# Output layers whose accumulators are added straight into the residual, and low parts made by ScalarE and an accumulating DMA

## The chip, the core and the metric

One NeuronCore of a Trainium2 chip runs one launch of the kernel. Its engines each run their own instruction stream in order: TensorE (PE; its weight loads are PEld), VectorE (DVE), ScalarE (ACT), GpSimd (POOL) and SyncE (SP, which here only issues DMAs). SBUF is the on-chip memory, PSUM holds matmul results, DRAM tensors hold inputs and spilled data. The metric is the device time of one launch in microseconds.

## The reference

One inference layer, on 1024 prompt tokens and 8 sample tokens together (1032 columns), model width 1024, in float32:

```python
x = layer_norm(ALPHA * x + 0.5 * swiglu(x, ffn1_wi, ffn1_wo), ln_g[0], ln_b[0])
...  # projections, mLSTM, short convolution, mixing: x <- LN2(...)
x = layer_norm(ALPHA * x + 0.5 * swiglu(x, ffn2_wi, ffn2_wo), ln_g[2], ln_b[2])
x = layer_norm(ALPHA * x + jax.nn.sigmoid(x @ w_pg) * (p @ w_pp), ln_g[3], ln_b[3])

def swiglu(x, wi, wo):
    g, u = jnp.split(x @ wi, 2, axis=-1)
    return (jax.nn.silu(g) * u) @ wo
```

The hidden width is 2816, that is 22 blocks of 128. The change concerns the second product of both SwiGLUs, `(...) @ wo`, called the output layer here.

## The kernel before

**Numbers in two pieces.** PE's matmuls take operands rounded to a shorter float (`fp32r`), so each operand is split: a high part, the rounded value, and a low part, value minus high part. A product is three matmuls: high times high, high times low, low times high (lines L432, L433, L434 of `product`; L172 to L174 in `unit`, the plain products). The low part of the activations is first needed by L433.

**Seven products for eight.** Most matrix products go by a Strassen-like scheme: a 256 x 256 weight block and two column halves of the data make seven products of sums instead of eight. `wcomb` forms the seven weight operands (copies of the high part on ACT, L258; low parts on DVE, L259; the sums on DVE, L267 and L270, and on POOL, L268 and L275). `pair` runs the seven products, j = 0 to 6, for each of two column strips s (256 and 260 columns), into PSUM accumulators: `mm` (four), `aux` (three), and one `pn` that `unit_ps` hands out every fifth time. Accumulator A takes products 0, 2 and 5, E takes 4 and 6; 1 and 3 go to `aux` tiles. Of A after 0, A after 2, product 3 and E after 4 a snapshot is copied to the SBUF tile `sreg` by ACT (L450, L457, L461, L465), and each of the four results per strip is a DVE sum of a snapshot and an accumulator (L454, L469, L470, L474).

**The output layer** in `ffn`. The hidden activations of eight (layer 1) or nine (layer 2) pairs of 128-blocks have been spilled as seven combined operands each, in the DRAM tensor `hsum`; a few blocks stay plain in `hscr`. Pairs are taken in groups of three (one group of two in layer 1). For a group, 7 x 3 = 21 *parts* of 128 x 516 are loaded by `split_load`: SP's DMA into the low half of a tile (L587), ACT's rounding copy to the high half (L588), DVE's subtraction (L589) in place over the low half. Then four `segment`s run, one for each 256 output rows: load `wo` (L603), `wcomb`, and `pair`. `out` has DVE write a result into a `tmp` tile and POOL add that to the residual tile `RT` (L610). Layer 1 has 8 pairs in three groups, layer 2 has 9 in three: 24 segments. The tiles of the parts are reused: product 0's parts of the next group may be loaded when PE has finished product 0 of the group's last segment, and so on, and in the next group they serve one product later. After the groups come the plain blocks (`ounit`, L632).

Every engine's order is fixed when the kernel is built: a list scheduler simulates the program and appends each instruction to its engine's stream, and an instruction waits for the semaphores of what it needs. So a late operand holds up all that stands behind it on that engine.

Of the kernel before, what the change touches and what calls it, by code (L numbers as in the profile page):

```python
# [11 lines left out]
AF = mybir.ActivationFunctionType  # L12
OP = mybir.AluOpType
# [17 lines left out]
BN = (256, 260)  # L31
BM = 260
BLK4 = [(i // 2 * HW + i % 2 * BN[0], BN[i % 2]) for i in range(4)]
# [3 lines left out]
def F_(ap):  # L37
    return ap.bitcast(F32)
# [25 lines left out]
def layer_kernel(ctx: ExitStack, tc: tile.TileContext, I, O):  # L64
    nc = tc.nc
    V, S, G, T, DQ = nc.vector, nc.scalar, nc.gpsimd, nc.tensor, nc.sync
# [28 lines left out]
    def tmp(n=BM):  # L95
        return tmpp.tile([128, BM], F32, name="tmp", tag="tmp")[:, :n]
# [6 lines left out]
    def unit_ps(n=512):  # L103

        turn["n"] += 1
        return mm(n) if turn["n"] % 5 else psp.tile([128, 512], F32, name="pn", tag="pn", bufs=1)[:, :n]
# [3 lines left out]
    def aux(n=512):  # L110
        return psp.tile([128, 512], F32, name="aux", tag="aux", bufs=7 - NMM)[:, :n]
# [71 lines left out]
    def bs(t, b, blk=BLK):  # L183
        c0, n = blk[b]
        return t[:, c0:c0 + n]
# [63 lines left out]
    def wcomb(raws):  # L249

        lo_, up = raws
        g = lo_.shape[1]
        a11, a21, a12, a22 = lo_[:, :, 0:128], lo_[:, :, 128:256], up[:, :, 0:128], up[:, :, 128:256]

        def put(src):
            s = slot()
            hi, lo = (s[:, i * 512:i * 512 + g * 128].rearrange("p (k n) -> p k n", n=128) for i in range(2))
            S.copy(hi, src)  # L258
            V.tensor_tensor(lo, src, F_(hi), op=OP.subtract)  # L259
            return hi, lo  # L260

        def fresh():
            return rawp.tile([128, 512], F32, name="raw", tag="raw")[:, :g * 128].rearrange("p (k n) -> p k n", n=128)

        s1, s2, s3 = fresh(), fresh(), fresh()
        out = [put(a11)]
        V.tensor_tensor(s1, a21, a22, op=OP.add)  # L267
        G.tensor_tensor(s3, a11, a21, op=OP.subtract)  # L268
        out.append(put(a12))
        V.tensor_tensor(s2, s1, a11, op=OP.subtract)  # L270
        out.append(put(s2))
        out.append(put(a22))
        out.append(put(s1))
        s4 = fresh()
        G.tensor_tensor(s4, a12, s2, op=OP.subtract)  # L275
        out.append(put(s3))
        out.append(put(s4))
        return out
# [150 lines left out]
    def product(ps, w, xs, start, stop):  # L429
        for kp, (xh, xl) in enumerate(xs):  # L430
            wh, wl = (t[:, kp] for t in w)
            T.matmul(ps, wh, xh, start=start and kp == 0, stop=False, skip_group_check=True)  # L432
            T.matmul(ps, wh, xl, start=False, stop=False, skip_group_check=True)  # L433
            T.matmul(ps, wl, xh, start=False, stop=stop and kp == len(xs) - 1, skip_group_check=True)  # L434
# [3 lines left out]
    def pair(ws, XS, subs, out, first=False):  # L438

        live = {}  # L440

        def step(j, s):
            w = ws[j]
            xs = XS(j, s) if callable(XS) else [xparts(XS[s], j, kp) for kp in range(4)]
            P = live.setdefault(s, {})
            snap = [SN["v"][i][s] for i in range(4)]
            if j == 0:
                P["A"] = mm(BN[s])
                product(P["A"], w, xs, True, False)
                order_["snap"] = S.copy(snap[0], P["A"]).ins  # L450
            elif j == 1:
                ps = aux(BN[s])
                product(ps, w, xs, True, True)
                out(0, s, lambda d: V.tensor_tensor(d, snap[0], ps, op=OP.add))  # L454
            elif j == 2:
                product(P["A"], w, xs, False, False)
                order_["snap"] = S.copy(snap[1], P["A"]).ins  # L457
            elif j == 3:
                ps = aux(BN[s])
                product(ps, w, xs, True, True)  # L460
                order_["snap"] = S.copy(snap[2], ps).ins  # L461
            elif j == 4:
                P["E"] = mm(BN[s])
                product(P["E"], w, xs, True, False)
                order_["snap"] = S.copy(snap[3], P["E"]).ins  # L465
            elif j == 5:
                A = P["A"]
                product(A, w, xs, False, True)
                out(1, s, lambda d: V.scalar_tensor_tensor(d, snap[2], -1.0, A, op0=OP.mult, op1=OP.add))  # L469
                out(1, s + 2, lambda d: V.tensor_tensor(d, snap[3], A, op=OP.add))  # L470
            else:
                E = P["E"]
                product(E, w, xs, False, True)
                out(0, s + 2, lambda d: V.tensor_tensor(d, snap[1], E, op=OP.add))  # L474


        for j, s in [(j, s) for js in ((0, 1), (2, 3, 4, 5, 6)) for s in subs for j in js] if first else \
                [(j, s) for j in range(7) for s in subs]:
            step(j, s)
            with tc.issue_after(order_["snap"]):  # L480
                for f in beside.pop(0) if beside else ():
                    f()

    def ffn(wi, wo, l, XS, enter, xlate, raws, sgs, RTs, res, groups, plains, tail, extra=None):
# [91 lines left out]
        for p in range(1, NHID // 2):  # L576
            for k in range(2):
                w = w0 if p == 1 and k == 0 else wcomb(wi_raw(p, k))
# [5 lines left out]
        def split_load(t, src):  # L584

            hi, lo = t
            DQ.dma_start(F_(lo), src)  # L587
            S.copy(hi, F_(lo))  # L588
            V.tensor_tensor(lo, F_(lo), F_(hi), op=OP.subtract)  # L589
            return hi, lo  # L590

        RT = []
# [5 lines left out]
        def segment(ps_, parts, n, i):  # L598
            g = len(ps_)
            rw = []  # L600
            for q in range(2):
                t = gen(raws[2 * (i % 2) + q])[:, :g * 256].rearrange("p (k n) -> p k n", n=256)
                DQ.dma_start(t, wo[ps_[0] * 256:(ps_[0] + g) * 256, n * 256:(n + 1) * 256].rearrange(  # L603
                    "(k t p) n -> t p k n", t=2, p=128)[q])
                rw.append(t)

            def out(i, c, fn):
                t, r = tmp(BN[c % 2]), bs(RT[2 * n + i], c, BLK4)
                fn(t)
                G.tensor_tensor(r, r, t, op=OP.add)  # L610

            pair(wcomb(rw), lambda j, s: [tuple(bs(u, s, BLK4) for u in parts[j, k]) for k in range(g)], (0, 1), out)

        i = 0
        for ps_, slots in groups:
            parts = {}
            for j in range(7):
                for k, p in enumerate(ps_):
                    t = gen(slots[j * len(ps_) + k], R)
# [14 lines left out]
        for gi, rows_ in enumerate(plains):  # L634
# [10 lines left out]
            else:  # L645
                if extra:
                    r = ring["slots"][ring["i"] % 9:] + ring["slots"][:ring["i"] % 9]
# [102 lines left out]
    ps = aux()  # L750
# [3 lines left out]
    ps = aux()  # L754
# [170 lines left out]
    def lin_store(dst, d, n, sm):  # L925
        for i in range(2):
# [5 lines left out]
            if sm is not None:  # L932
# [6 lines left out]
    parts = {0: [(0, 26, 27), (1, 0, 1)], 2: [(7, 31, 32), (6, 10, 11)],  # L939
             1: [(0, 2, 3), (1, 8, 9)], 3: [(7, None, None), (6, 28, 29)]}  # L940
# [13 lines left out]
    for c in (0, 2, 1, 3):  # L954
        for k in range(2):
            for i in range(2):
                if len(wp) < 4:
                    wp.append(wcol(w_in, (Q0, K0)[k] + i * 128))
                ps = unit_ps(BLK4[c][1])
# [477 lines left out]
    ps = aux()  # L1437
# [314 lines left out]
    for t, nm in ((gB, "ln_g"), (bB, "ln_b")):  # L1752
        src = I[nm][0, 3]
# [61 lines left out]
```

## Time and profile before

| | us |
|---|---|
| median of 3 runs | 2705.56 (2703.46 to 2705.6) |
| the profiled execution | 2706.57 |
| its span, first to last instruction | 2704.8 |
| PE busy | 2647.3 (98%) |
| DVE busy | 1856.5 (69%) |
| ACT busy | 1341.6 (50%) |
| POOL busy | 830.1 (31%) |

All stretches below are microseconds from the span's start. Layer 1's output layer runs from about 461 to 645, layer 2's from about 2317 to 2515. In the groups of instructions, a row has line, engine, operation, tiles (out<-in, numbers left out), shapes and count, then the busy time, the mean ns of one, and the idle time of that engine just before with what ended it. In a row of one line's instructions stand the minimum, median and maximum in ns and the first and last start. In the table by stretches each engine has its busy time and, in brackets, its number of instructions; then PE's granted clock, the share of DMA and its GB/s. A wait's row has the total, the number and the longest. Matmuls overlap in their pipeline, so their rate is read from counts, not from the duration of one.

### The profile page before, as it was taken

What the parts mean: (1) busy time and instruction counts of PE and PEld (TensorE: products, weight loads), DVE (VectorE), ACT (ScalarE), POOL (GpSimd) and SP (SyncE); (2) the same over time, 40 slices, a digit from 0 to 9 for tenths busy, and PEclk for the clock granted to TensorE, in tenths of its full rate; (3) what the DMA queues carried; (4) which work ended last, traced back from release to release, by engine and by line L of the source; (5) the groups of instructions that cost most, each with busy time, mean ns of one, the idle gap of its engine ahead of it and who ended that gap; (6) DMA issues with size and microseconds to landing.
All of it is one profiled execution on the core that took longest, in us unless ns stands there. A gap on an engine that the chain in (4) does not pass through costs nothing.

```text
span 2704.8 us, 56720 instructions
## 1 busy us (share of the span) xinstructions
PE 2647.3 (98%) x21775; PEld 2610.3 (97%) x21775; DVE 1856.5 (69%) x3932; ACT 1341.6 (50%) x3031; POOL 830.1 (31%) x840
## 2 busy tenths in 40 slices
PE   9999999999999999999999999999999999999998
PEld 9999999999999999999999999999999999999888
DVE  6755556887885756646666677758855555788887
ACT  5544446554554445446666555425544444655351
POOL 2222221565421111111111334323322222465554
PEclk9999999999999999999999999999999999999999
DMA  6333236432332434236657776731433323643211
GB/s 206 103 108 107 89 104 209 145 120 69 102 107 88 122 98 126 79 88 181 183 176 230 244 231 220 249 100 32 161 100 106 102 90 109 214 150 119 81 46 58
DMA packets 311928, 355.18 MB, mean 131 GB/s; under 512 B 28536, under 2 KB 246344, under 8 KB 311656
## 3 DMA queue, kind: packets, MB, share of 16 engines
q1 hardware_dynamic: 289336, 330.30, 38.4%
q10 hardware_dynamic: 22320, 21.26, 2.7%
q8 instruction: 170, 2.79, 0.4%
q14 instruction: 102, 0.84, 0.1%
HBM read 246.09 MB, written 105.42 MB: 130 GB/s over the span
## 4 chain that ended last, share of the span: by engine, by line
PE 37%; DVE 6%; DMA 4%; issue 2%; ACT 2%; POOL 1%; SPq 0%; DVEq 0%; ACTq 0%; POOLq 0%
PE mm L432 5%; PE mm L433 5%; PE mm L434 5%; PE mm L172 4%; PE mm L174 4%; PE mm L173 4%; PE aux L433 2%; PE aux L434 2%; PE aux L432 2%; PE pn L174 1%; PE pn L172 1%; DMA a<-in_w_in_dram 1%; PE pn L173 1%; DVE a L212 1%; DMA a<-yscr 1%
## 5 line engine op out<-in xcount | busy, mean ns | idle before, releaser
L432 PE MATMUL mm<-a,w 128*128 128x256 f32 (+1 forms) x2402 | 680.5, 284 | 9.4 <-DVE tmp L470 5.9
L433 PE MATMUL mm<-a,w 128*128 128x256 f32 (+1 forms) x2402 | 676.8, 282 | 1.2 <-DVE a L212 1.2
L434 PE MATMUL mm<-a,w 128*128 128x256 f32 (+1 forms) x2402 | 675.2, 281 | 0.0
L432 PEld LDWEIGHTS mm<-a,w 128*128 128x128 f32 x2402 | 452.6, 188 | 15.9 <-DVE tmp L470 7.6
L433 PEld LDWEIGHTS mm<-a,w 128*128 128x128 f32 x2402 | 453.0, 189 | 2.1 <-DVE a L212 1.6
L434 PEld LDWEIGHTS mm<-a,w 128*128 128x128 f32 x2402 | 452.6, 188 | 0.1
L275 POOL TENSOR_TENSOR raw<-a,raw 128x512 f32<-128x512 f32 (+2 forms) x98 | 125.4, 1279 | 949.5 <-issue 443.9
L259 DVE TENSOR_TENSOR w<-raw,w 128x512 fp32r<-128x512 f32 (+2 forms) x258 | 185.6, 721 | 203.5 <-ACT w L258 201.1
L432 PE MATMUL aux<-a,w 128*128 128x260 f32 (+1 forms) x1000 | 283.1, 283 | 3.9 <-DVE a L454 3.0
L433 PE MATMUL aux<-a,w 128*128 128x260 f32 (+1 forms) x1000 | 282.1, 282 | 0.0
L434 PE MATMUL aux<-a,w 128*128 128x260 f32 (+1 forms) x1000 | 282.1, 282 | 0.0
L432 PE MATMUL mm<-a,e 128*128 128x256 f32 (+1 forms) x812 | 230.1, 283 | 1.6 <-DVE tmp L474 1.1
L433 PE MATMUL mm<-a,e 128*128 128x256 f32 (+1 forms) x812 | 229.0, 282 | 0.8 <-DVE a L212 0.8
L434 PE MATMUL mm<-a,e 128*128 128x256 f32 (+1 forms) x812 | 228.6, 281 | 0.0
L610 POOL TENSOR_TENSOR a<-a,tmp 128x256 f32<-128x256 f32 (+1 forms) x192 | 178.9, 959 | 86.8 <-DVE tmp L454 37.8
L174 PE MATMUL mm<-a,w 128*128 128x256 f32 (+4 forms) x715 | 201.5, 285 | 0.0
L172 PE MATMUL mm<-a,w 128*128 128x256 f32 (+3 forms) x671 | 191.7, 287 | 4.0 <-ACT w L148 1.7
L432 PEld LDWEIGHTS aux<-a,w 128*128 128x128 f32 x1000 | 188.9, 189 | 5.4 <-DVE a L454 4.0
L258 ACT CAST w<-a 128x512 fp32r<-128x512 f32 (+2 forms) x200 | 117.5, 587 | 149.7 <-PE mm L434 93.6
L173 PE MATMUL mm<-a,w 128*128 128x256 f32 (+3 forms) x671 | 190.6, 285 | 0.0
L434 PEld LDWEIGHTS aux<-a,w 128*128 128x128 f32 x1000 | 189.1, 189 | 0.0
L433 PEld LDWEIGHTS aux<-a,w 128*128 128x128 f32 x1000 | 189.1, 189 | 0.0
(508 smaller groups left out, 7790.9 us busy)
## 6 DMA issues: line engine op xcount, KB each, us to landing
a<-in_ffn_wi_dram SPq DMA_DIRECT2D x80, 512.0 KB
a<-in_w_in_dram SPq DMA_DIRECT2D x68, 512.0 KB
a<-hsum SPq DMA_DIRECT2D x119, 258.0 KB
hsum<-a SPq DMA_DIRECT2D x68, 258.0 KB
a<-in_ffn_wo_dram SPq DMA_DIRECT2D x40, 384.0 KB
a<-in_state_C_dram ACTq DMA_DIRECT2D x32, 256.0 KB
out_dram<-a ACTq DMA_DIRECT2D x32, 256.0 KB
raw<-in_w_b_dram SPq DMA_DIRECT2D x32, 256.0 KB
```

The lines of the kernel that those rows point to most:

```text
L172: T.matmul(ps, wh, xh, start=(i == 0), stop=False)
L173: T.matmul(ps, wh, xl, start=False, stop=False)
L174: last = T.matmul(ps, wl, xh, start=False, stop=(i == n - 1))
L212: order_["lo"] = V.tensor_tensor(dst[1], src, F_(dst[0]), op=OP.subtract).ins
L258: S.copy(hi, src)
L259: V.tensor_tensor(lo, src, F_(hi), op=OP.subtract)
L275: G.tensor_tensor(s4, a12, s2, op=OP.subtract)
L432: T.matmul(ps, wh, xh, start=start and kp == 0, stop=False, skip_group_check=True)
L433: T.matmul(ps, wh, xl, start=False, stop=False, skip_group_check=True)
L434: T.matmul(ps, wl, xh, start=False, stop=stop and kp == len(xs) - 1, skip_group_check=True)
L610: G.tensor_tensor(r, r, t, op=OP.add)
```

## The change

Two edits, both in `ffn`.

1. In a segment, `pair`, `out`, `tmp`, the snapshots and POOL's adds go. Each accumulator is added straight from PSUM into the residual by DVE as it stands after each product: 8 adds for each strip, 16 for each segment (product 5's twice), with high priority. A and E come from `unit_ps`, products 1 and 3 from `aux`.
2. In `split_load` the subtraction on DVE goes. ACT writes minus the high part over the low half, and a DMA that POOL issues adds the same DRAM source to it.

```diff
             hi, lo = t
             DQ.dma_start(F_(lo), src)
             S.copy(hi, F_(lo))
-            V.tensor_tensor(lo, F_(lo), F_(hi), op=OP.subtract)
+            S.activation(lo, F_(hi), AF.Copy, scale=-1.0)
+            G.dma_start(F_(lo), src, accum_op=OP.add)
             return hi, lo
...
-            def out(i, c, fn):
-                t, r = tmp(BN[c % 2]), bs(RT[2 * n + i], c, BLK4)
-                fn(t)
-                G.tensor_tensor(r, r, t, op=OP.add)
-
-            pair(wcomb(rw), lambda j, s: [tuple(bs(u, s, BLK4) for u in parts[j, k]) for k in range(g)], (0, 1), out)
+            w = wcomb(rw)
+
+            def add(i, c, ps, op=OP.add):
+                r = bs(RT[2 * n + i], c, BLK4)
+                with tc.high_priority():
+                    V.tensor_tensor(r, r, ps, op=op)
+
+            A, E = {}, {}
+            for j, s in [(j, s) for j in range(7) for s in range(2)]:
+                if j in (0, 4):
+                    (E if j else A)[s] = unit_ps(BN[s])
+                ps = (aux(BN[s]) if j % 2 and j < 5 else E[s] if j in (4, 6) else A[s])
+                product(ps, w[j], [tuple(bs(u, s, BLK4) for u in parts[j, k]) for k in range(g)],
+                        j not in (2, 5, 6), j not in (0, 2, 4))
+                if j == 3:
+                    add(1, s, ps, OP.subtract)
+                elif j == 5:
+                    add(1, s, ps)
+                    add(1, s + 2, ps)
+                else:
+                    add(int(j == 4), s + 2 if j in (2, 4, 6) else s, ps)
```

Lines of the new kernel: L588 is still the copy of the high part, L589 is now ACT's negation, L590 POOL's DMA.

The scheduler makes another order of this. The places shown are at layer 1's first change of group (about 509 us in the profile before); `a_` numbers are tile instances, and differ between the two kernels for the same part. ACT before, from the first reused part (a_6845) on; e and w are weight operands:

```order
L588 CAST a_6845<-a_6845 128x516
L258 CAST e_6936<-a_6919 128x384
L588 CAST a_6849<-a_6849 128x516
L457 COPY sreg<-mm 128x256
L588 CAST a_6853<-a_6853 128x516
L588 CAST a_6857<-a_6857 128x516
L457 COPY sreg<-mm 128x260
L258 CAST w_6939<-raw 128x384
```

ACT now, from the same part (a_6805) on:

```order
L588 CAST a_6805<-a_6805 128x516
L589 ACTIVATE a_6805<-a_6805 128x516
L588 CAST a_6810<-a_6810 128x516
L258 CAST e_6914<-a_6897 128x384
L588 CAST a_6815<-a_6815 128x516
L589 ACTIVATE a_6810<-a_6810 128x516
L588 CAST a_6820<-a_6820 128x516
L258 CAST w_6917<-raw 128x384
L589 ACTIVATE a_6815<-a_6815 128x516
```

The snapshots (L457) are gone and the negations stand among the copies. POOL before, in the same place, has weight sums and residual adds:

```order
L275 TENSOR_TENSOR raw<-a_6919,raw 128x384
L268 TENSOR_TENSOR raw<-a_7116 128x384
L610 TENSOR_TENSOR a_5950<-a_5950,tmp 128x256 x2
L610 TENSOR_TENSOR a_5950<-a_5950,tmp 128x260 x2
L610 TENSOR_TENSOR a_5947<-a_5947,tmp 128x256
```

and now:

```order
L590 DMA a_6815<-hsum_91 128x516
L275 TENSOR_TENSOR raw<-a_6897,raw 128x384
L590 DMA a_6820<-hsum_91 128x516
L268 TENSOR_TENSOR raw<-a_7078 128x384
L590 DMA a_6825<-hsum_91 128x516
L590 DMA a_6830<-hsum_91 128x516
```

Fifteen accumulating DMAs in a row, the last two rows the first of them, stand here before POOL's next sum. PE before, at the last three reused parts (a_6905 to a_6913), product 6 of the next group's first segment:

```order
L434 MATMUL mm<-a_6901,w_6944 128x260
L432 MATMUL mm<-a_6905,w_6947 128x256
L433 MATMUL mm<-a_6905,w_6947 128x256
L434 MATMUL mm<-a_6905,w_6947 128x256
L432 MATMUL mm<-a_6909,w_6947 128x256
L433 MATMUL mm<-a_6909,w_6947 128x256
```

and now (a_6880 is the part a_6905 was; e_7105 is a weight of the second segment):

```order
L433 MATMUL mm<-a_6870,e_7105 128x256
L433 MATMUL mm<-a_6875,w_6922 128x256
L434 MATMUL mm<-a_6875,w_6922 128x256
L433 MATMUL mm<-a_6875,w_6922 128x260
L434 MATMUL mm<-a_6875,w_6922 128x260
L434 MATMUL mm<-a_6870,e_7105 128x256
L432 MATMUL mm<-a_6875,e_7105 128x256
L433 MATMUL mm<-a_6875,e_7105 128x256
L432 MATMUL pn<-a_6880,w_6925 128x256
```

PE goes through the parts one at a time, with both strips and products of the second segment in between, where it took a whole product of nine matmuls before the next.

## The prediction

> **What bounds the kernel now.** First the page: totals of each engine and the 40 slices (each 67.6 us).
>
> ```profile
> span 2704.8 us, 56720 instructions
> PE 2647.3 (98%) x21775; PEld 2610.3 (97%) x21775; DVE 1856.5 (69%) x3932; ACT 1341.6 (50%) x3031; POOL 830.1 (31%) x840
> ...
> DVE  6755556887885756646666677758855555788887
> ACT  5544446554554445446666555425544444655351
> ```
>
> TensorE (PE) is busy 98%, so the change, which leaves its matmuls as they are, can gain only idle time of PE. The output layers lie in slices 7 to 10 and 35 to 38, where VectorE (DVE) mostly reads 7 and 8. Second, the table by stretches: for each, PE's busy time and matmuls.
>
> ```profile
> core 0: us, PE busy (x) PEld busy (x) DVE busy (x) ACT busy (x) POOL busy (x), PEclk, DMA share, GB/s
> 2100.00:2150.00 50.00, 50.00 (x423) 50.00 (x422) 26.47 (x54) 20.75 (x47) 10.58 (x9) 1.00 0.27 85
> 461.00:482.00 21.00, 20.78 (x173) 20.36 (x172) 20.70 (x36) 16.42 (x35) 8.36 (x8) 1.00 0.83 297
> 505.00:545.00 40.00, 37.73 (x315) 37.31 (x314) 36.93 (x61) 24.10 (x55) 23.06 (x23) 1.00 0.55 179
> 575.00:605.00 30.00, 26.64 (x213) 25.46 (x212) 29.37 (x45) 21.11 (x49) 16.24 (x17) 1.00 0.56 194
> 605.00:645.00 40.00, 38.92 (x312) 37.35 (x313) 32.53 (x61) 18.17 (x43) 27.88 (x33) 1.00 0.34 107
> 2365.00:2396.00 31.00, 29.43 (x241) 28.65 (x240) 26.71 (x44) 20.77 (x48) 12.87 (x14) 1.00 0.64 214
> 2428.00:2460.00 32.00, 29.76 (x247) 29.35 (x247) 29.07 (x48) 21.01 (x48) 15.72 (x15) 1.00 0.60 202
> ```
>
> The first row is PE undisturbed: 50/423 = 0.1182 us per matmul. What a stretch lasts beyond its count times 0.1182 is lost: 0.5 us at the start of layer 1's output (461), 2.8, 2.5 and 2.8 us at three changes of group (505, 2365, 2428), 4.8 us at the fourth (575) and 3.1 us in layer 1's tail (605). At the changes DVE is busy 86 to 98% and DMA works hardest: the next group's parts are loaded there. The waits of PE in 500 to 645 name DVE, not DMA:
>
> ```profile
> PE mm L432 <- DVE tmp L470: 3.5, 5, 1.2
> PE mm L432 <- DVE tmp L474: 1.8, 2, 1.1
> PE aux L432 <- DVE tmp L454: 0.9, 1, 0.9
> ```
>
> So at stake is 0.5 + 8.1 + 4.8 = 13.4 us, and little of the tail's 3.1.
>
> **The evacuation.** Groups of instructions by line and shape:
>
> ```profile
> L610 POOL TENSOR_TENSOR a<-a,tmp 128x260 f32<-128x260 f32 x96 | 95.2, 1002 | 7.2 <-DVE tmp L469 4.0 <-DVE tmp L454 3.0
> L589 DVE TENSOR_TENSOR a<-a 128x516 fp32r<-128x516 f32 x119 | 95.2, 818 | 18.6 <-ACT a L588 17.8
> L461 ACT COPY sreg<-aux 128x260 f32<-128x260 f32 x98 | 37.0, 377 | 64.9 <-PE aux L434 64.1 <-issue 0.7
> L259 DVE TENSOR_TENSOR w<-raw,w 128x384 fp32r<-128x384 f32 x52 | 36.8, 711 | 18.0 <-ACT w L258 18.0
> L454 DVE TENSOR_TENSOR tmp<-sreg,aux 128x260 f32<-128x260 f32 x52 | 21.8, 419 | 9.4 <-PE aux L434 9.2
> L258 ACT CAST w<-raw 128x384 fp32r<-128x384 f32 x52 | 27.0, 520 | 19.9 <-POOL raw L275 12.8 <-DVE raw L270 7.1
> ...
> L211 ACT CAST a<-a 128x256 fp32r<-128x256 f32 x112 | 43.4, 406 | 24.6 <-DVE a L1174 22.9 <-DVE st L1093 0.6 <-PE pn L1188 0.6
> ```
>
> There are 24 segments. Each loses 8 snapshots on ScalarE (ACT), 8 DVE sums into tmp and 8 POOL adds, and gains 16 DVE adds from PSUM into the residual, priced like L454 (a PSUM and an SBUF operand, same width). ACT: 192 x 0.377 = -72 us. POOL: 192 adds at 1.0 us, -190 us. DVE: +192 x 0.419 = +80 us, and -119 x 0.818 = -97 us for the low parts that leave it. None of it lies on PE's path except where PE waited for DVE above. The new read before PE accumulates on (product 0's add before product 2) has three products between, 27 matmuls or 3.2 us for groups of three, against an add of 0.42 us; I cost it at nothing. If DVE's queue runs more than 2.8 us late that cover is gone, and DVE's load falls.
>
> **The low parts.** Per part, DVE's subtraction (0.69 us at best) becomes an ACT negation, a wait of POOL for it, and an accumulating DMA that fetches the part from DRAM a second time; SP's plain load stays. What PE now waits for is a DMA behind ACT. The rows at the first change of group, 509 to 540:
>
> ```profile
> L587 SPq DMA_DIRECT2D a<-hsum x21: 319/382/1358, 509.4 to 524.4; - x21
> ...
> L588 ACT CAST a<-a x21: 619/627/652, 513.2 to 531.1; 128x516 fp32r<-128x516 f32 x21
> ...
> L589 DVE TENSOR_TENSOR a<-a x21: 680/689/1506, 513.8 to 538.6; 128x516 fp32r<-128x516 f32 x21
> ...
> GB/s 169 307 101 296 397 312 314 360 362 322 365 373 405 386 230 233 323 260 381 341 314 280 392 392 389 187 3 11 164 301 42 0 21 0 0 0 0 0 0 0
> DMA packets 4223, 6.77 MB, mean 218 GB/s; under 512 B 384, under 2 KB 1532, under 8 KB 4220
> ```
>
> (the last two rows are DMA's rate in 40 slices of 0.775 us and its total in that stretch.)
>
> A load takes 3.8 us from issue (509.4) to ACT's copy (513.2), and DMA runs at 300 to 400 GB/s for 20 us: already full. The order of ACT after the change (shown under the change) holds two passes per part where it held one: from the first reused part's copy to the last of 18 negations it has 21 copies, 18 negations and 10 casts: 39 x 0.627 + 10 x 0.52 = 29.7 us. Begun at 513.2, that ends at 542.9; an accumulate as quick as a load (3.8 us) lands at 546.7.
>
> The scheduler has moved PE's need back too (the rows of PE under the change). PE now takes parts one at a time with the next segment's products between. From PE's release of the last reused part's slot to its first need of the low part the order had 134 matmuls and has 202. Counted from the first release (509.4) the last need is 298 matmuls on: 509.4 + 298 x 0.1182 = 544.6. So even with cheap accumulates the last part is 546.7 - 544.6 = 2.1 us late.
>
> The accumulate's price no row shows. At least it moves what a load moves, 128 x 516 x 4 bytes = 0.264 MB; at most it reads both operands one after the other and costs two loads, 0.528 MB. With two, DMA moves 6.77 + 18 x 0.528 = 16.3 MB; at 400 GB/s (the better slices) 40.7 us from 509, and 1 us to land (an estimate): 550.7, 6.1 us late. I take two: the destination must be fetched too, and DMA is full here. The Trainium skill, "Collectives: The Full Stack", section "The bandwidth ceiling: the fold count and why AG ≠ RS ≠ AR", says an adding transfer pushes two reads through the same ring and measured half the rate; no run here shows that, and it would give the same 6.1 us.
>
> Three changes of group follow this pattern: 3 x 6.1 = 18.3 us late in place of the 8.1 us lost now, **+10.2**. Start of layer 1's output, where ACT and DMA are fuller still (ACT's residual scaling, and 442 to 472):
>
> ```profile
> 442.00:472.00 30.00, 30.00 (x255) 30.00 (x254) 23.44 (x48) 25.73 (x51) 4.32 (x4) 1.00 1.00 355
> ...
> DMA packets 5109, 10.66 MB, mean 355 GB/s; under 512 B 488, under 2 KB 1514, under 8 KB 5107
> ...
> L588 ACT CAST a<-a x20: 608/627/662, 445.1 to 475.3; 128x516 fp32r<-128x516 f32 x20
> ...
> L587 SPq DMA_DIRECT2D a<-hsum x21: 319/320/339, 442.5 to 475.6; - x21
> ...
> L596 ACT ACTIVATE a<-a x16: 1067/1076/1098, 453.6 to 2337.6; 128x1032 f32<-128x1032 f32 x16
> ```
>
> PE needs the last part 351 matmuls after the first release, 442.5 + 41.5 = 484.0. DMA: 10.66 MB less 1.2 MB that is for later, plus 19 x 0.528: 19.5 MB, 48.8 us, 492.3 with landing: 8.3 us late, less 0.5, **+7.8**. ACT alone: 38 x 0.627 + 8 x 1.076 + 9 x 0.377 + 10 x 0.52 = 41.0 us from 445.1, plus 3.8: 489.9, 5.9 us late. Layer 1's second change of group (573 to 605) has 11 short and 4 double-length accumulates ahead of its need:
>
> ```profile
> DMA packets 3124, 6.39 MB, mean 200 GB/s; under 512 B 304, under 2 KB 1072, under 8 KB 3119
> ...
> L587 SPq DMA_DIRECT2D a<-hsum x11: 319/381/587, 572.0 to 584.8; - x11
> ...
> L588 ACT CAST a<-a x16: 617/633/1082, 574.7 to 592.5; 128x516 fp32r<-128x516 f32 x11, 128x1032 fp32r<-128x1032 f32 x5
> ```
>
> Without the fifth long part, which is for later, 5.9 + 11 x 0.528 + 4 x 1.057 = 15.9 MB: 39.7 us from 573, 613.7 with landing; the need is 237 matmuls after the first load's issue at 572.0, 600.0: 13.7 us late, less 4.8, **+8.9**. Layer 2's start has 366 matmuls of cover (43.3 us, 1.8 more than layer 1's) and its residual scaling (L596) runs as late as 2337.6, behind the parts: **0**. On POOL the accumulates stand in a row with the weight sums (L268, L275). The tightest is the next segment's fourth sum, behind the 19th accumulate: begun at about 543, its weight is ready by 547 (1.2 us of sum, copy and split), and PE needs it 351 matmuls after the first release, at 551: nothing. On SP, part loads stand behind weight loads that wait for these sums to free a buffer; the one among this change's loads waits only for the third accumulate: nothing. Sum: 10.2 + 7.8 + 8.9 = **+27 us**. The profiled execution took 2706.57 us, the median of the runs is 2705.56; I forecast 2706 + 27 = **2733 us**.
>
> **Rivals.** (1) No change: an accumulate costs one load. ACT alone sets lateness: 3 x 2.1 - 8.1 = -1.8; 5.9 - 0.5 = +5.4; at the second change 22 x 0.627 + 8 x 1.08 + 13 casts of 256 columns at 0.406 (L211) = 27.7 us from 574.7, plus 3.8: 606.2, 6.2 late, less 4.8 = +1.4. Sum +5, 2711; 0.2% is 5.4 us, about what a measurement here tells from nothing. The Trainium skill, "DMA: Bandwidth & Descriptors", section "Anatomy of one DMA — SWDGE (gpsimd) path", fits 2.0 us plus size over 436 GB/s for one transfer of POOL's queue: an estimate of 2.6 us where I have 3.8 from the row, by which this rival's sum would be about -1 us; no run here shows it yet.
>
> (2) Faster: the parts come in time and PE's losses go, 13.4 plus some of the tail's, -15, 2690. It decides if accumulates land within 1.7 us of their negation (544.6 - 542.9) at every change. For it: DVE's weight splits (L259) run 711 ns on average beside POOL's adds, which leave. Against it: ACT's 29.7 us at a change.
>
> (3) Much slower: POOL's issue of an accumulate is the bound. SP's issue takes 0.32 to 0.38 us, POOL's own adds 1.0; 18 issues exceed DMA's 41 us only above 1.9 us each. At 3 us: 514.4 + 54 + 3.8 = 572, 27.6 late at three changes, 25 more each, and some 20 at the other two places: +115, 2820.
>
> **How the numbers follow.** Forecast 0.42, rival 1 0.22, faster 0.15, rival 3 and accumulates of three loads (each change 18 us late instead of 6, about +80) together 0.21. The forecast's own range is 2715 to 2752. The range over the cases is 2694 to 2770: it cuts the far ends of the faster and of the much slower case. Faster by over 0.2% 0.15, within 0.2% 0.22, slower 0.63.
>
> **What would show it.** PE waits at L433 in 461 to 645 and 2317 to 2460 on a DMA into a from hsum, 5 to 14 us per change; waits on L470 gone there; ACT's L588 and L589 back to back at 513 to 543; DMA full for 40 us, not 20; bytes up by 33 to 37 MB or double that. Wrong if DMA's busy time at a change ends by 540, or if PE waits on ACT or on POOL instead.

## The result: slower, by three times the forecast

The changed kernel took 2792.06 us (median; 2788.42 to 2800.46) beside 2705.58 us for the kernel before: a ratio of 1.0325, 95% interval 1.0303 to 1.0346, 86 us slower. The forecast was 2733 us with a range to 2770. The direction was right, and so were five of the six places; the size was not, and the sixth place had been set at nothing.

The page of the new kernel (totals, PE's row of the 40 slices, and DMA's totals):

```profile
span 2791.5 us, 56628 instructions
PE 2668.3 (96%) x21775; PEld 2627.2 (94%) x21775; DVE 1795.1 (64%) x3995; ACT 1358.9 (49%) x2968; POOL 757.4 (27%) x777
...
PE   9999998888999999999999999999999999888898
...
DMA packets 330505, 391.91 MB, mean 140 GB/s; under 512 B 30601, under 2 KB 248409, under 8 KB 330233
```

PE has the same 21775 matmuls and a span 86.7 us longer; DVE has less work than before (64% where it had 69%). The six places of the prediction, by the table of stretches (the stretches are those of the new kernel's own times):

```profile
core 0: us, PE busy (x) PEld busy (x) DVE busy (x) ACT busy (x) POOL busy (x), PEclk, DMA share, GB/s
440.00:505.00 65.00, 51.06 (x382) 48.22 (x380) 24.24 (x56) 41.37 (x77) 22.43 (x25) 0.92 1.02 278
528.00:580.00 52.00, 41.37 (x302) 40.62 (x301) 23.99 (x55) 29.80 (x57) 22.44 (x25) 0.87 1.03 240
604.00:655.00 51.00, 36.81 (x275) 34.96 (x274) 24.36 (x66) 28.23 (x50) 17.79 (x21) 0.87 0.98 236
2337.00:2398.00 61.00, 46.99 (x360) 45.38 (x360) 25.18 (x58) 39.54 (x76) 24.26 (x27) 0.92 1.06 288
2423.00:2474.00 51.00, 38.91 (x296) 37.63 (x295) 22.67 (x53) 29.59 (x57) 22.40 (x25) 0.87 1.05 246
2499.00:2549.00 50.00, 40.96 (x316) 40.59 (x316) 25.74 (x59) 29.31 (x55) 21.70 (x24) 0.90 1.01 239
```

With 0.1182 us for each matmul, the rows lose 19.8, 16.3, 18.5, 18.4, 16.0 and 12.6 us: 101.6 us, where the prediction counted 13.4 before (with nothing at layer 2's start, where 515 matmuls took 61.00 us). The difference of 88 us is about the whole change of the span (86.7). The rest of the program shifts by a few us that nearly cancel: by the same matmuls, 6.8 us less are lost between the two output layers and 4.4 us more behind the second. In each row DMA's share is 0.98 to 1.06: it is full for 50 to 65 us at a time, and DVE is busy about half of that or less. The waits of PE over the whole span, longest first:

```profile
PE aux L432 <- ACT a L589: 20.2, 3, 8.1
PE mm L433 <- DMA a<-hsum: 12.3, 9, 6.2
PE mm L432 <- ACT w L258: 8.2, 3, 4.1
PE pn L432 <- DVE a L613: 7.5, 1, 7.5
PE mm L172 <- DVE a L648: 6.7, 5, 4.1
PE aux L433 <- DMA a<-hsum: 6.0, 5, 3.1
PE mm L432 <- DVE a L613: 4.8, 6, 1.7
PE aux L432 <- DVE a L613: 4.3, 5, 1.8
```

The wait that the prediction named, L433 on an accumulating transfer, is only 18 us of it. The other names are ACT and DVE: for instance a weight (L258) or a PSUM tile that DVE's add (L613) has yet to empty. A name in such a row needs care: L432 doesn't read what L589 writes. The longest wait of the table, just before 2464 us, in order of time (start and duration in us; in brackets the engine's idle time before, and what ended it):

```profile
2462.56 0.51 ACT L258 CAST cd<-a 128x384 fp32r<-128x384 f32 x1
...
2463.10 0.56 DVE L259 TENSOR_TENSOR cd<-a,cd 128x384 fp32r<-128x384 f32 x1 [13.11 <-ACT cd L258]
...
2463.58 0.75 DVE L613 TENSOR_TENSOR a<-a,aux 128x256 f32<-128x256 f32 x2
2464.14 0.55 PE L432 MATMUL aux<-a,w 128*128 128x256 f32 x1 [8.14 <-ACT a L589]
```

PE starts when DVE's add has emptied the `aux` tile. That add stood on DVE behind a weight split, the split waited 13 us for a cast on ACT, and the cast stood behind part copies (L588) that waited for their loads. The wait of 5.7 us that ended at 569.5 has the same sequence. So it looked as if standing in line on ACT made PE late; one experiment below tests it.

### The profile page after: what moved, and what is told of

It reads as the page before. It is cut to its first block, busy times and chain, and to the rows that moved or that the text cites. A ratio compares the mean times of both kernels' runs of the same rounds, so it can differ in the third digit from the quotient of the medians.

```text
span 2791.5 us, 56628 instructions
## 1 busy us (share of the span) xinstructions
PE 2668.3 (96%) x21775; PEld 2627.2 (94%) x21775; DVE 1795.1 (64%) x3995; ACT 1358.9 (49%) x2968; POOL 757.4 (27%) x777
## 2 busy tenths in 40 slices
DMA packets 330505, 391.91 MB, mean 140 GB/s; under 512 B 30601, under 2 KB 248409, under 8 KB 330233
## 3 DMA queue, kind: packets, MB, share of 16 engines
q0 software_dynamic: 18576, 36.73, 7.5%
HBM read 282.82 MB, written 105.42 MB: 139 GB/s over the span
## 4 chain that ended last, share of the span: by engine, by line
PE 71%; DMA 15%; DVE 7%; ACT 3%; issue 2%; POOL 1%; SPq 0%; ACTq 0%; DVEq 0%; POOLq 0%
PE mm L432 12%; PE mm L433 12%; PE mm L434 12%; PE aux L432 5%; PE aux L433 5%; PE aux L434 5%; PE mm L172 5%; PE mm L174 5%; PE mm L173 5%; DMA a<-hsum 3%; DMA a<-hscr 2%; DVE a L212 1%; DMA a<-in_w_in_dram 1%; PE pn L173 1%; PE pn L172 1%
## 5 line engine op out<-in xcount | busy, mean ns | idle before, releaser
L432 PE MATMUL mm<-a,w 128*128 128x256 f32 (+1 forms) x2313 | 656.3, 285 | 18.5 <-ACT w L258 8.2
L433 PE MATMUL mm<-a,w 128*128 128x256 f32 (+1 forms) x2313 | 654.3, 283 | 13.4 <-DMA a<-hsum 12.3
L434 PE MATMUL mm<-a,w 128*128 128x256 f32 (+1 forms) x2313 | 651.8, 282 | 0.0
L432 PEld LDWEIGHTS mm<-a,w 128*128 128x128 f32 x2313 | 437.2, 189 | 25.3 <-ACT w L258 8.8
L433 PEld LDWEIGHTS mm<-a,w 128*128 128x128 f32 x2313 | 438.3, 190 | 16.3 <-DMA a<-hsum 14.7
L434 PEld LDWEIGHTS mm<-a,w 128*128 128x128 f32 x2313 | 438.2, 190 | 0.1
L275 POOL TENSOR_TENSOR raw<-a,raw 128x512 f32<-128x512 f32 (+2 forms) x98 | 125.7, 1282 | 919.7 <-issue 421.5
L259 DVE TENSOR_TENSOR w<-raw,w 128x512 fp32r<-128x512 f32 (+2 forms) x258 | 177.1, 687 | 240.0 <-ACT w L258 235.5
L432 PE MATMUL aux<-a,w 128*128 128x260 f32 (+1 forms) x1000 | 284.0, 285 | 19.9 <-ACT a L589 13.9
L433 PE MATMUL aux<-a,w 128*128 128x260 f32 (+1 forms) x1000 | 283.5, 284 | 4.3 <-DMA a<-hsum 4.3
L432 PE MATMUL mm<-a,e 128*128 128x260 f32 (+1 forms) x785 | 222.6, 284 | 2.6 <-ACT a L588 2.5
L433 PE MATMUL mm<-a,e 128*128 128x260 f32 (+1 forms) x785 | 221.7, 283 | 1.0 <-DVE a L212 0.8
L434 PE MATMUL mm<-a,e 128*128 128x260 f32 (+1 forms) x785 | 221.3, 282 | 0.0
L432 PEld LDWEIGHTS aux<-a,w 128*128 128x128 f32 x1000 | 190.2, 190 | 22.1 <-ACT a L589 17.0
L174 PE MATMUL mm<-a,w 128*128 128x256 f32 (+3 forms) x739 | 208.8, 285 | 0.2 <-DVE w L149 0.2
L172 PE MATMUL mm<-a,w 128*128 128x260 f32 (+4 forms) x695 | 199.0, 287 | 6.9 <-DVE a L648 5.9
L173 PE MATMUL mm<-a,w 128*128 128x260 f32 (+4 forms) x695 | 197.8, 286 | 0.0
L433 PEld LDWEIGHTS aux<-a,w 128*128 128x128 f32 x1000 | 190.8, 191 | 5.0 <-DMA a<-hsum 5.0
L258 ACT CAST w<-a 128x512 fp32r<-128x512 f32 (+2 forms) x200 | 117.1, 586 | 157.5 <-PE mm L434 95.2
L258 ACT CAST w<-raw 128x512 fp32r<-128x512 f32 (+2 forms) x258 | 152.4, 591 | 58.6 <-PE mm L434 27.4
```

The lines of the kernel that those rows point to most:

```text
L172: T.matmul(ps, wh, xh, start=(i == 0), stop=False)
L173: T.matmul(ps, wh, xl, start=False, stop=False)
L174: last = T.matmul(ps, wl, xh, start=False, stop=(i == n - 1))
```

## The experiments

Twelve kernels, each timed beside the kernel before (medians of 2701 to 2706 us). In the comparisons of places, "lost" is worked out as above.

**Edit 1 alone.**

```diff
-            S.activation(lo, F_(hi), AF.Copy, scale=-1.0)
-            G.dma_start(F_(lo), src, accum_op=OP.add)
+            V.tensor_tensor(lo, F_(lo), F_(hi), op=OP.subtract)
```

> Edit 1 alone: accumulators are added straight into the residual, the low parts are again the subtraction on VectorE. Theory: edit 1 is harmless or a small gain, and all of the loss of 86 us sits in the low parts: at the changes of group the losses of before (2.8, 4.8, 2.5 and 2.8 us) shrink with VectorE's load, so 2690 to 2704 us. Rival: the new order of TensorE (one part at a time, two segments interleaved) is itself what makes it wait, because it needs a part's low half sooner: then 2730 us or more without any accumulating transfer.

2691.19 us, ratio 0.9953 (0.9935 to 0.9972): faster than both kernels, so the loss isn't edit 1's. The rival is not settled by this run: with the subtraction back, the scheduler doesn't make the interleaved order. By the traces, in the changed kernel 162 of the L433 matmuls don't stand right behind the L432 of their own product, here 44, in the kernel before 34. The narrow kernel below keeps that order. Two of DVE's groups (subtraction, and the 384-wide weight splits) fit the gain:

```profile
L589 DVE TENSOR_TENSOR a<-a 128x516 fp32r<-128x516 f32 x119 | 86.1, 737 | 17.0 <-ACT a L588 16.7
...
L259 DVE TENSOR_TENSOR w<-raw,w 128x384 fp32r<-128x384 f32 x52 | 28.9, 559 | 4.2 <-ACT w L258 4.2
```

737 ns for a subtraction that took 818 before, 559 for a split that took 711: without POOL's residual adds beside them, DVE's own instructions are shorter.

**Edit 2 alone.** The reverse: the kernel before, with the two lines of `split_load` from the change.

> Edit 2 alone: snapshots, tmp and GpSimd's residual adds stay, the low parts come from ScalarE's negation and the accumulating transfer. Theory: the loss of 86 us is here whole, and more, since GpSimd's adds (1.0 us each) now stand between the accumulating transfers, and ScalarE's snapshots among the passes: 2790 to 2830 us. Rival (edit 1's order of TensorE is to blame): 2750 us or less.

2804.95 us, ratio 1.0382 (1.0365 to 1.0400), 103 us over the kernel before. So the edits nearly add up: 103 - 11 is 92, and both together gave 86. The loss is edit 2's, and so is most of the new order of PE (109 L433 matmuls away from their L432).

**A plain transfer, and a narrow one.** Two kernels with everything of the change but the adding, or but the bytes:

```diff
-            G.dma_start(F_(lo), src, accum_op=OP.add)
+            G.dma_start(F_(lo), src)                                            # plain
+            G.dma_start(F_(lo)[:, 0:4], src[:, 0:4], accum_op=OP.add)           # narrow
```

> The changed kernel with GpSimd's transfer made a plain one: it overwrites the low half with the source where it added to it (the low halves are then wrong numbers). Every instruction, wait and order is the same; only the adding is gone. Theory of price: in 520 to 590 us of the changed kernel the accumulating queue held DMA for 46% of 70 us for 21 parts, 1.53 us each, against 0.66 us for a load at 400 GB/s. With a plain transfer 18 parts take 13 to 15 us less of DMA at each change, so the six places lose 50 to 60 us less in all: 2730 to 2745 us. Theory of the chain: it isn't what the transfer costs DMA, but that a second transfer stands behind copy, negation and GpSimd's issue, each part 9 us after the other: then 2775 us or more.

> The changed kernel with the accumulating transfer cut to the first 4 of 516 columns (the other columns keep minus the high part). The waits and the instructions stay, DMA's bytes for it go; the order of instructions shifts in places. Theory of price: DMA is then as free as before, ScalarE's two passes are what is left, by the working of the first rival 5 us over the kernel before or less: 2700 to 2715 us. Theory of the chain: a transfer still has to be issued by GpSimd and land after the negation, so most of the loss stays: 2750 us or more.

Plain: 2723.53 us, ratio 1.0074 (1.0059 to 1.0089). Narrow: 2681.43 us, ratio 0.9919 (0.9904 to 0.9933). The plain kernel has every instruction of the changed one in the same order, so the adding alone costs 2792 - 2724 = 68 us. The narrow one keeps all instructions and, up to shifts, the interleaved order of PE (153 L433 away from their L432); its 4 columns lie in the first strip, so only that strip's matmuls read what the transfer writes. It is the fastest kernel of the study: that order, the negation and POOL's issue cost PE next to nothing. Its row for the first change of group:

```profile
508.00:545.00 37.00, 37.00 (x314) 37.00 (x313) 25.41 (x58) 29.78 (x59) 22.40 (x25) 1.00 0.71 194
```

314 matmuls in 37.00 us are 0.1178 each: nothing lost, with ACT as busy as in the changed kernel (29.8 us) and DMA at 0.71. Apart from the second strip's wait the chain is that of the changed kernel; what differs is what DMA carries. The queue of POOL's transfers on the pages of the changed kernel and of the plain one (packets, MB, share of 16 engines):

```profile
q0 software_dynamic: 18576, 36.73, 7.5%
```

```profile
q0 software_dynamic: 10960, 36.73, 3.8%
```

The same bytes take 0.075 x 2791.5 = 209 us of all 16 engines with adding and 0.038 x 2722.6 = 103 us without: twice. With 119 single and 10 double parts that is 1.51 and 0.74 us a part. The Trainium skill, "Collectives: The Full Stack", section "The bandwidth ceiling: the fold count and why AG ≠ RS ≠ AR", says of the adding step of a reduction between cores that it reads two sources through one ring and gets half the rate; this trace agrees (2.0 times), here within one core and with the old value in SBUF.

**Half the columns.**

```diff
+            n = src.shape[-1] // 2
+            G.dma_start(F_(lo)[:, 0:n], src[:, 0:n], accum_op=OP.add)
```

> The changed kernel with the accumulating transfer over the first half of the columns (the other half keep minus the high part; the order of instructions shifts somewhat). The plain transfer of all columns held DMA for 3.8% of 16 engines' span, 0.74 us a part, the accumulating one 7.5%, 1.5 us, and gave 2724 and 2792 us. Theory (what counts is DMA's time, by bytes moved twice): half the columns are 0.75 us a part and give what the plain one gives, 2715 to 2735 us. Rival (a price for each row's packet, whatever its size, 144 packets a part in both): 1.2 us or more a part, 2755 us or more.

2724.55 us, ratio 1.0078 (1.0060 to 1.0097), what the plain transfer of all columns gave. Its queue:

```profile
q0 software_dynamic: 18576, 18.37, 4.5%
```

0.045 x 2724.2 = 123 us, 0.88 us a part: near the theory's 0.75, well under the rival's 1.2, with as many packets as in the changed kernel. The narrow kernel's queue (also 18576 packets, 0.27 MB, 1.1%) held DMA for 29 us, 0.21 a part. So 0.2 of the 1.51 us don't go with the bytes, and 1.3 do. What counts is mostly bytes; "adding counts twice" is what a whole part measures, not a law for any size.

**Two plain transfers in a row.** The accumulating line replaced by two plain ones.

> The changed kernel with two plain transfers of the part, one after the other on GpSimd's queue, in place of the accumulating one (the low halves are wrong; the order of instructions shifts). One plain transfer gave 2724 us, the accumulating one 2792. Theory of DMA's time: two plain ones of 0.74 us a part hold DMA as long as an accumulating one of 1.5: 2775 to 2805 us. Rival (adding costs more than a second transfer does, by waiting inside the transfer for the old value): the two plain ones overlap and cost less, 2765 us or less.

2814.05 us, ratio 1.0409 (1.0391 to 1.0426): above the theory's window, and far from the rival. The page has both:

```profile
q0 software_dynamic: 21920, 73.46, 7.1%
```

0.071 x 2806.4 = 199 us, nearly as much of DMA as the accumulating queue's 209. The 22 us more than the changed kernel aren't DMA's amount. The second transfer writes over the first and has to wait for it, and POOL's queue with it: before the second transfers POOL stood idle 47 us for a landing, which the changed kernel doesn't do. That this wait makes the 22 us was not tried. For the same reason the rival was not put to the test: the two transfers of a part could not overlap.

**ScalarE's negation left out.** The line `S.activation(lo, F_(hi), AF.Copy, scale=-1.0)` is dropped.

> The changed kernel without ScalarE's negation: the accumulating transfer adds to the plain load (low halves are then twice the value, wrong). ScalarE loses 119 passes of 0.63 us, 18 of them at each change of group, 11 us there. Theory (only DMA's amount counts, since DMA is full all through the change): 2775 to 2795 us, as the changed kernel. Rival (ScalarE's passes and DMA's time come one after the other, so that both lengthen the chain): 18 x 0.63 us at six places come off at least in half, 2755 us or less.

2808.17 us, ratio 1.0388 (1.0367 to 1.0409). Nothing of the rival's gain shows. But it is 16 us slower than the changed kernel, which the theory didn't expect either: its order shifts, and PE waits 64 us for a PSUM tile that DVE's add has yet to empty, against 17. Why is open, so this run doesn't measure the passes alone. That they are not what makes PE late is shown by the narrow kernel, which has them all.

**Weight casts out of ScalarE's line.** In the output layers `wcomb` has DVE make the high parts.

```diff
-            w = wcomb(rw)
+            w = wcomb(rw, V.tensor_copy)
```

> The changed kernel with the output layers' weight casts (L258, 168 of them) on VectorE instead of ScalarE; everything else is kept. In the changed kernel TensorE's long waits at the changes of group are mostly at L432, not at L433: for a weight or a PSUM tile that hangs on a weight cast, which on ScalarE stands behind part copies that wait for late loads (4.2 and 5.9 us at 555 and 569, 7.6 at 2379, 8.4 at 2464, 2.8 and 6.5 at 2524 and 2537). Theory of the queue: a good part of the 86 us is this standing in line; with the casts out of it 25 us or more come back, 2767 us or less. Theory of DMA's amount: the parts themselves are late by as much, and TensorE waits for them at L433 instead: 2785 to 2800 us.

2792.93 us, ratio 1.0334 (1.0316 to 1.0352): no change at all. The theory of the queue falls. Its waits of PE:

```profile
PE pn L432 <- DVE a L613: 16.3, 3, 8.3
PE mm L433 <- DMA a<-hsum: 15.9, 10, 7.5
PE mm L432 <- DVE a L613: 9.3, 5, 6.1
PE aux L433 <- DMA a<-hsum: 8.4, 9, 2.7
...
PE pn L433 <- DMA a<-hsum: 3.9, 4, 1.7
```

The waits for a weight cast are gone, and those at L433 have grown from 18 to 28 us, those for a PSUM tile (L613) from 17 to 26: the same time under other names. The line on ACT is not what makes PE late.

**A third of the parts.** Edit 1, with the accumulating transfer for the first pair of each group only, 42 parts; the others have DVE's subtraction.

> Edit 1 whole, edit 2 for one part in three (the first pair of each group); the other parts have VectorE's subtraction. Theory of a threshold: DMA has some slack at a change of group (with the accumulating transfers cut to 4 columns the kernel took 2681 us), and a third of them, 6 or 7 of 1.5 us, fit in it: 2683 to 2697 us, as edit 1 alone (2691). Rival, a loss in proportion: a third of the 101 us between edit 1 alone and both edits: 2720 to 2728 us.

2703.75 us, ratio 1.0000 (0.9988 to 1.0012). Both miss: there is no free third, and it costs less than its share (13 of 101 us over edit 1 alone). The price rises with the dose. From edit 1 alone to a third, 65 us of DMA's time (2.4% of 2700.2; 1.54 us a part) cost 13 us, 0.2 for one (a little more by itself, since 42 subtractions leave DVE too); from the narrow transfer (29 us) to the plain one (103) 74 us cost 42, 0.6 for one; from the plain to the adding one 106 us more cost 68, 0.65 for one.

**The residual's loads left out.** ScalarE fills the residual tiles from a constant instead of scaling loaded ones.

```diff
-            DQ.dma_start(RT[m], res[m])
-            S.activation(RT[m], RT[m], AF.Copy, scale=ALPHA)
+            S.activation(RT[m], ones[:, 0:1].to_broadcast([128, NT]), AF.Copy, scale=ALPHA)
```

> The changed kernel without the loads of the residual (8 of 0.53 MB at the start of each layer's output; ScalarE fills the tiles with a constant in the same number of passes, so the residual is left out; the order of instructions shifts). Theory (at the starts too DMA's amount is the bound, and the residual's loads take their share of it): at each start 7 to 8 loads, 3.7 to 4.2 MB, go, 10 us at the 373 GB/s that DMA moved there with the adding transfers counted twice; the starts lose some 8 us each where they lost 19.5, in all 2765 to 2778 us. Rival (each part's own chain of load, passes and adding transfer is too long for the cover, whatever else DMA does): 2785 us or more.

2775.33 us, ratio 1.0270 (1.0244 to 1.0296), in the theory's window. Loads that the change doesn't touch give back 17 us when they go: about 7 at the start of layer 1's output and 8 at that of layer 2's, by when the matmul of the same number starts. Part of it may be waits for the residual itself: in the changed kernel the one wait of 7.5 us for `pn` is for an add of DVE that waits for ScalarE's scaling of a residual tile. The two weren't separated.

**Towards a faster kernel.** Edit 1 alone beats both kernels, and the narrow kernel, 10 us faster still without DVE's subtractions, suggests that the rest lies there. Two tries, each on edit 1 alone: a third of the subtractions on POOL, and the output layers' weight sums (L268, L275) on DVE in place of POOL.

```diff
+                    parts[j, k] = split_load((t[:, 0:HW], t[:, HW:NT]), hsum[j, p], G if k == 2 else V)
```

```diff
+            w = wcomb(rw, V)      # G's two sums in wcomb on V
```

> Edit 1, with the subtraction of one part in three (the third pair of a group) on GpSimd, the others on VectorE; no accumulating transfer. Edit 1 frees 190 us of GpSimd. A subtraction of 516 columns should take it about 2 us (its adds of 260 columns took 1.0), 7 parts 14 us at a change of group. Theory: VectorE's subtractions are what still holds TensorE in edit 1 alone, since the kernel with 4-column transfers, which has no subtraction at all, is 10 us faster: 2680 to 2688 us. Rival: GpSimd is late with them or with the weight sums behind them, and slows VectorE where both run: 2692 us or more.

> Edit 1 alone (VectorE's subtraction), with the output layers' two weight sums per segment that GpSimd does (L268, L275; 1.1 to 1.2 us each) on VectorE (0.55 us each, 48 of them, 26 us). A third of the subtractions on GpSimd cost 18 us against edit 1 alone, so work on GpSimd beside VectorE is dear. Theory: without any GpSimd work in the output layers VectorE keeps its 0.55 us for each split and weights are ready sooner: 2682 to 2689 us. Rival: VectorE is what holds TensorE there, and 26 us more on it cost: 2693 us or more.

The first took 2709.5 us, ratio 1.0027 (1.0017 to 1.0037), 18 us worse than edit 1 alone. Its groups:

```profile
L589 DVE TENSOR_TENSOR a<-a 128x516 fp32r<-128x516 f32 x84 | 72.9, 878 | 17.7 <-ACT a L588 17.6
L589 POOL TENSOR_TENSOR a<-a 128x516 fp32r<-128x516 f32 x35 | 53.4, 1529 | 111.3 <-ACT a L588 76.0 <-PE aux L434 12.7 <-PE mm L434 12.2
...
L259 DVE TENSOR_TENSOR w<-raw,w 128x384 fp32r<-128x384 f32 x52 | 35.9, 691 | 4.9 <-ACT w L258 4.8
```

POOL takes 1.5 us, and DVE's subtractions rise from 737 to 878 ns, its splits from 559 to 691. The second took 2686.58 us, ratio 0.9946 (0.9927 to 0.9965): faster than the kernel before, inside its theory's window, but not to be told from edit 1 alone. Its subtractions took 685 ns and its splits 549, shorter again with less work on POOL.

## Why the prediction missed

**What held.** Its mechanism: adding counts as two loads (measured 2.0 of a plain transfer), DMA is the bound at the places, the bytes shown rise once (391.91 - 355.18 = 36.73 MB; forecast 33 to 37), PE's waits for L470 are gone there, POOL's queue is no bound (an issue took 0.865 us in the median, under the 1.9 us that rival 3 needed), and the new read between products costs nothing (edit 1 alone gained 11 us). The two loads of the sum were the upper of two bounds, chosen by an argument; they came out, though that the second half of the time is the fetch of the old value no row shows. Rival 1 is refuted by the price; and with its price, a plain transfer, the kernel took 2724 us, not its 2711, so that its sum was too small in the same way. The rival of a faster kernel is what comes about where DMA carries nothing more: the narrow transfer, 2681. Rival 3 is refuted by POOL's row:

```profile
L590 POOL DMA_DIRECT2D a<-hsum x119: 856/865/1896, 429.5 to 2538.7; - x119
```

**The step that failed: the time that DMA needs for the sum of bytes.** The forecast divided by 400 GB/s, "the better slices", and took PE's cover off. Its 1 us to land was an estimate that no row shows by itself. What DMA moved at the first change of group, in 40 slices of 1.275 us and by queue:

```profile
GB/s 156 256 382 355 340 256 217 264 270 251 256 261 257 261 264 256 258 239 254 238 249 256 298 257 298 261 254 264 361 230 185 62 149 152 154 168 192 199 163 224
...
q0 software_dynamic: 2916, 5.37, 61.1%
q1 hardware_dynamic: 4422, 6.92, 42.6%
```

Three phases can be read in the row: loads alone (to 382), loads and accumulating transfers nearly in halves (536 to 565: 4.15 and 3.42 MB, which is 379 GB/s with adding counted twice), and at the end, after a slice at 62, mostly accumulating transfers (565 to 580: 0.50 and 2.04 MB, 305 GB/s). Over the 51 us that is 6.92 + 2 x 5.37 = 17.7 MB, 346 GB/s. The same two rows for the start of layer 1's output (441 to 502), its second change (604 to 650), the start of layer 2's output (2337.9 to 2395) and its first change (2423 to 2474):

```profile
q1 hardware_dynamic: 5921, 12.22, 58.3%
q0 software_dynamic: 2867, 5.27, 47.3%
```

```profile
q0 software_dynamic: 2171, 5.08, 60.3%
q1 hardware_dynamic: 3239, 6.44, 42.4%
```

```profile
q1 hardware_dynamic: 5663, 11.63, 58.2%
q0 software_dynamic: 2702, 4.98, 47.9%
```

```profile
q0 software_dynamic: 2978, 5.48, 61.8%
q1 hardware_dynamic: 4528, 7.02, 43.0%
```

They make 22.8, 16.6, 21.6 and 18.0 MB in 61, 46, 57.1 and 51 us: 373, 361, 378 and 353 GB/s. The prediction's own quoted row for 442 to 472, with a DMA share of 1.00, had 355: the mean of a full stretch, which was there to be used. With its own bytes and 355 in place of 400, the forecast's lateness is 11.3 us at each of the three changes, 14.4 at layer 1's start and 18.9 at its second change: +54 us in place of +27. Of the 86 us, 27 more are then explained by the rate alone. Taking 355 and the bytes that really went in the stretch:

| place | cover of PE, us | MB, adding twice (forecast) | at 355 GB/s, us | late | lost, measured | late, forecast |
|---|---|---|---|---|---|---|
| layer 1, start | 41.5 | 22.8 (19.5) | 64.2 | 22.7 | 19.8 | 8.3 |
| first change of group | 35.2 | 17.7 (16.3) | 49.9 | 14.7 | 16.3 | 6.1 |
| layer 1, second change | 28.0 | 16.6 (15.9) | 46.8 | 18.8 | 18.5 | 13.7 |
| layer 2, start | 43.3 | 21.6 (not summed) | 60.8 | 17.5 | 18.4 | 0 |
| layer 2, first change | 35.2 | 18.0 (16.3) | 50.7 | 15.5 | 16.0 | 6.1 |

(Cover: the prediction's count of matmuls from the first release of a slot to the last need, times 0.1182. The stretches end where the waits end, and DMA is full throughout, so bytes over rate give back nearly the stretch's own length: the table shows that the account is consistent. It is no proof; that the amount is the cause is shown by the narrow, plain, half and residual-free kernels.) Lateness is a small difference between two large times. Layer 2's second change, the sixth place, lost 12.6. At the first change DMA's time rose from the forecast's 41 to some 50 us, a fifth, and what stuck out over the cover of 35 us from 6 to 16.

Second, **layer 2's start was set at nothing** from PE's cover and from one late residual scaling, without a sum of its bytes. It has 21.6 MB to move, the residual's loads among them, and loses 18.4 us: after the rate the largest part of what was missing. The kernel without those loads lost some 8 us less there.

Third, **bytes for later count too.** The forecast took 1.2 MB off at layer 1's start and left out the next products' accumulating transfers because PE needs them later. DMA does not wait for that: what is issued shares it. 19.5 MB became 22.8, 16.3 became 17.7.

Fourth, **the names of the waits.** The forecast looked for L433 alone, 5 to 14 us per change; 18 us of it stood there in all, the rest at weights and PSUM tiles. Its own sign of being wrong, that PE waits on ACT, came about by name: some 39 us of PE's waits at the six places are put down to ACT. The experiment with DVE's casts shows that the name says little: ACT and DVE go through their instructions in order, so a late load holds whatever is behind it. ACT's passes weren't back to back, as forecast, but waited for loads, 78 us before L588 in all:

```profile
L588 ACT CAST a<-a 128x516 fp32r<-128x516 f32 x119 | 72.8, 620 | 78.2 <-DMA a<-hsum 78.0
```

Of the gains, DVE fell by 61 us where the sum had 17: its splits became shorter (all 686 of them from 504 to 471 us; the 384-wide from 711 to 564 ns), as in edit 1 alone, and the 10 double-length subtractions, which the sum left out, went too. There the gain at PE was 11 us; here it is lost under the late loads.

## What to carry to other kernels

Before moving work from a compute engine to a transfer, sum what DMA has to carry in the stretch between the slot's release and the need, everything that is issued in it, adding transfers twice (as they measured here, with rows of 2 KB), and divide by the rate of a stretch that is wholly full, not by its best slices. Where that is near PE's cover, each further microsecond of DMA comes out more and more as a wait (0.2 to 0.65 us here), under whatever name the in-order engines give it. Test such a suspicion by keeping every instruction and cutting the bytes: it separates the amount from the chain in one run.

## What the runs showed of the hardware

The clock of PE falls after a long wait. The end of the first change's last long wait, in stretches of 5 us:

```profile
565.00:570.00 5.00, 0.48 (x2) 0.51 (x3) 1.51 (x4) 4.80 (x11) 2.03 (x3) 0.80 0.93 155
570.00:575.00 5.00, 5.00 (x26) 5.00 (x25) 2.64 (x4) 1.37 (x3) 5.00 (x6) 0.52 1.05 168
575.00:580.00 5.00, 5.00 (x44) 5.00 (x44) 4.45 (x11) 1.44 (x3) 0.27 (x1) 1.00 0.98 184
```

PE is busy all through 570 to 575 and does 26 matmuls where it does 44 in the next 5 us; the granted clock is 0.52. The Trainium skill, "TensorE: Matmul & The Clock Gate", section "HAM oscillation — how this bites in real kernels", says that gaps of more than about 3.4 us in PE's work bring the half clock back; the 4 to 8 us waits here agree. A sharp limit doesn't show: the half clock also followed waits of 2.1, 2.7 and 2.9 us (ending at 2588.7, 2523.8 and 2673.9), and a wait of 3.1 us (ending at 2358.0) left the clock full. Summed over the matmuls of the trace that started at the half clock, what they took above 0.1185 us (gaps over 0.25 us counted as 0.25) is 22 us in the changed kernel and 5 in the one before. The forecast had no such term. At the six places it is 17 us. So much of their loss may be the clock and not the waits; no run separates them.

An accumulating transfer's destination does not show in the bytes: the page counts 36.73 MB for it with and without adding, and only the share of the engines' time (7.5 and 3.8%) and the packets (18576 and 10960) tell them apart. What was read from HBM is 282.82 MB in both.
